# Mirrored RWKV solve, feed-forward loads issued one by one, and another scheduling model in a two-layer hybrid trunk

## The chip, the core and the metric

The kernel runs on one core of a Trainium2 chip. TensorE (PE) multiplies matrices and writes to PSUM; its weight loads (PEld) overlap its matmuls. DVE (VectorE), ACT (ScalarE) and POOL (GpSimd) compute on vectors. DMA engines move data between HBM and SBUF; here nearly all transfers are issued by SP (SyncE). Each engine works through its own queue of instructions in order, and waits where an operand is not ready. The metric is the device time of one execution in microseconds (us), lower is better.

## The reference

Two layers follow each other. In each, 256 tokens of width 1024 are projected by `w_in`; three mixers work on parts of the projection, their outputs are weighted by sigmoid gates and added, and an output projection, a feed-forward block and two layer norms follow. All of it is causal and in float32.

```
p = x @ w_in[l]
y_a = rwkv7_time_mix(p[..., :o_mla], ...)        # 8 heads of 64
y_b = mla_branch(p[..., o_mla:o_s5], ...)        # 8 heads, causal attention
y_c = s5_branch(p[..., o_s5:o_gate], ...)        # 32 groups, 64 states, gelu, GLU
merged = gates[..., 0, :] * y_a + gates[..., 1, :] * y_b + gates[..., 2, :] * y_c
x = layer_norm(DEEPNORM_ALPHA * x + merged @ w_out[l], ln1_g[l], ln1_b[l])
h = jax.nn.silu(x @ ffn_w1[l]) * (x @ ffn_w3[l])
x = layer_norm(DEEPNORM_ALPHA * x + h @ ffn_w2[l], ln2_g[l], ln2_b[l])
```

The RWKV mixer is a recurrence over the tokens. With a state of 64 x 64 per head, one step is

```
sa = jnp.einsum('bhvk,bhk->bhv', state, a_t)
state = state * w_t[:, :, None, :] + sa[..., None] * b_t[:, :, None, :] + v_t[..., None] * k_t[:, :, None, :]
y_t = jnp.einsum('bhvk,bhk->bhv', state, r_t)
```

## The kernel before, in words

**Weights.** All weights come as chunks of 128 x 1024 numbers (512 KB), 138 per layer. `w_load` (L156) issues the transfer into one of three buffers `raw` on SP (L160), rounds the chunk to `whi` on ACT (L161), and forms the remainder `wlo` on DVE (L171; in the first third of a layer a part of it on POOL, L173). There are four pairs of `whi` and `wlo`, and chunks are prepared four ahead of their use. The activations are split in the same way, so that a product in float32 is three matmuls: `xh` with `whi` (L206), `xl` with `whi` (L207) and `xh` with `wlo` (L208). The second projections of a block, with 512 columns, have such triplets at L510 to L512. All of these are called projections here.

**Order.** For each layer two lists, `ORDER1` and `ORDER2`, name the steps in program order: `S` and `r` are projections for S5 and RWKV, `P` and `N` the latents of the attention and their norm, `t` the S5 scan, `p`, `s`, `i`, `j`, `v`, `n` RWKV's preparation, scores, the two parts of the inverse, the solve and the norm, `a` and `b` attention, `l` the GLU and `o`, `h` the outputs of the mixers. From the program the scheduler of the language makes one queue per engine; it may set instructions in another order than the program has them, where the data allow it.

**RWKV.** The eight heads lie in four tiles `f`, two heads to a tile, and two tiles make a pair `g`, in which `e` counts the tiles. `prep` (L858) makes, for one tile, decays and keys: two matmuls (L867, L871), tanh on ACT, scans and products on DVE (L877 to L910, among them `kk`, L893, which reads `pa` from the transposes at L891), transposes of `BK` and `vT` (L916, L921). `scores` (L931) forms `Mk` (L940, copied by ACT, masked by POOL, L947). `inverse` (L951) copies blocks of `Mk` to `P` (on ACT), runs 15 dependent steps of three small DVE operations (L968 to L970), and then builds blocks of 64 (L983 to L1011). `solve` (L1018) has four dependent steps: matmuls of `Mk` with `ST` (L1035, from the second step on with the state, L1031), a copy to `Gc` on ACT, matmuls with the inverse (L1043), a copy into `ST` on DVE, and the update of the state (L1053, L1055, scaled on DVE at L1059). In each step both tiles of the pair use the same rows and columns of the array. L1067 and L1070 then make the output.

**S5.** `s5_tables` (L348) computes tables of powers of the poles; `rotation` runs on POOL, the complex products `cmul` (L404 to L409) on DVE in layer 0, and `spread` (L418, on ACT in layer 0) makes `bd` and `cd`. `s5_in` (L685) copies `u` into the layout `U` with eight transfers (L695) on SP.

**Output projection and second feed-forward projection.** Both are `token_major` (L497), with 8 and 22 chunks. At step `at` of its loop (2 and 12) it issues three transfers on SP: the norm's scale `lg` and shift `lb`, 512 KB each, and the residual `xk`, 1 MB.

The lines of the changed kernel are about 6 higher up to the RWKV part and about 20 higher after it.

## Time and profile before

| | before |
|---|---|
| median of 3 runs | 1072.03 us (1067.92 to 1077.68) |
| the profiled execution | 1068.97 us, its span 1067.1 us |
| PE busy | 1014.2 us, 95% |
| PE weight loads busy | 912.5 us, 86% |
| DVE busy | 784.7 us, 74% |
| ACT busy | 482.6 us, 45% |
| POOL busy | 235.2 us, 22% |
| moved by DMA | 163.86 MB, mean 154 GB/s |

A busy time is the time in which at least one instruction of the engine runs. Matmuls overlap, so the mean time of one is longer than its distance to the next. The page's list of groups has one row for each line, engine and tile: how often, busy us and mean ns, and behind the bar how long the engine stood idle just before them and what ended that. The granted clock (PEclk) is a share of PE's full speed.

### The profile page before, as it was taken

The page shows a single profiled execution, that of the slowest core. Times are in us where ns is not written, and L with a number is a line of the kernel's source. Part 1 is how long each engine was busy: PE and PEld are TensorE (multiplying, and loading weights), DVE is VectorE, ACT ScalarE, POOL GpSimd, SP SyncE. Part 2 cuts the span into 40 slices and gives each one's busy share as a digit, 9 for nine tenths or more (in the row PEclk, how much of TensorE's full clock was granted, in tenths as well). Part 3 has the DMA queues.
Part 4 walks back from the last instruction along what each step waited for, and adds up shares of the span by engine and source line. Part 5 has one row for each costly group of instructions (what it writes and reads, how often), then busy time and mean ns, then how long its engine had stood idle before and what let it go on. Part 6 is the DMA issues. An engine that isn't in the chain of part 4 may idle for free.

```text
span 1067.1 us, 21219 instructions
## 1 busy us (share of the span) xinstructions
PE 1014.2 (95%) x8560; PEld 912.5 (86%) x8560; DVE 784.7 (74%) x1542; ACT 482.6 (45%) x797; POOL 235.2 (22%) x262
## 2 busy tenths in 40 slices
PE   8799989999999999799999999999999999999997
PEld 7798778888896999798878999778889879999885
DVE  7969978976578778386474998888747876667546
ACT  5544477534244244144325346865334423443431
POOL 2970222300000599500012003221002420000000
PEclk9989999999999999999999999999999999999999
DMA  8442241223385555466536325232234755555562
GB/s 280 156 159 90 91 147 41 92 89 100 93 294 177 197 180 171 162 207 217 185 123 218 126 81 191 79 98 85 76 100 173 252 190 215 183 188 183 179 196 79
DMA packets 47394, 163.86 MB, mean 154 GB/s; under 512 B 5696, under 2 KB 8256, under 8 KB 46400
## 3 DMA queue, kind: packets, MB, share of 16 engines
q1 hardware_dynamic: 47008, 161.98, 45.9%
q8 instruction: 67, 1.10, 0.4%
q10 hardware_dynamic: 288, 0.52, 0.1%
q14 instruction: 31, 0.25, 0.1%
HBM read 156.72 MB, written 4.19 MB: 151 GB/s over the span
## 4 chain that ended last, share of the span: by engine, by line
PE 58%; DVE 17%; POOL 9%; DMA 7%; ACT 5%; issue 3%; SPq 0%; DVEq 0%; ACTq 0%; POOLq 0%
PE mm L208 11%; PE mm L207 10%; PE mm L206 10%; DMA raw<-in_ws 6%; DVE wlo L171 3%; PE mm L511 3%; PE mm L512 3%; PE mm L510 3%; ACT whi L161 3%; DVE z L745 1%; PE pa L726 1%; PE pb L1035 1%; POOL st L387 1%; PE pb L1043 1%; PE pa L940 1%
## 5 line engine op out<-in xcount | busy, mean ns | idle before, releaser
L171 DVE TENSOR_TENSOR wlo<-raw,whi 128x1024 fp32r<-128x1024 f32 (+2 forms) x265 | 333.5, 1262 | 171.8 <-ACT whi L161 169.1
L161 ACT CAST whi<-raw 128x1024 fp32r<-128x1024 f32 (+2 forms) x267 | 277.4, 1043 | 379.8 <-PE mm L207 211.8
L206 PE MATMUL mm<-xh,whi 128*128 128x256 f32 x1312 | 376.9, 287 | 14.2 <-ACT whi L161 13.9
L208 PE MATMUL mm<-xh,wlo 128*128 128x256 f32 x1312 | 376.1, 287 | 2.9 <-DVE wlo L171 2.6
L207 PE MATMUL mm<-xl,whi 128*128 128x256 f32 x1312 | 375.1, 286 | 0.4 <-DVE xl L262 0.4
L206 PEld LDWEIGHTS mm<-xh,whi 128*128 128x128 f32 x1312 | 249.2, 190 | 18.6 <-ACT whi L161 14.5
L208 PEld LDWEIGHTS mm<-xh,wlo 128*128 128x128 f32 x1312 | 250.2, 191 | 7.6 <-DVE wlo L171 4.0
L207 PEld LDWEIGHTS mm<-xl,whi 128*128 128x128 f32 x1312 | 250.2, 191 | 2.7 <-DVE xl L262 0.6
L240 POOL TENSOR_TENSOR rs<-rs,mhalf 128x1 f32<-128x1 f32 x8 | 7.8, 971 | 341.2 <-DVE rs L238 341.2
L206 PE MATMUL mm<-yh,whi 128*128 128x256 f32 x256 | 74.6, 291 | 0.1
L207 PE MATMUL mm<-yl,whi 128*128 128x256 f32 x256 | 74.1, 289 | 0.0
L208 PE MATMUL mm<-yh,wlo 128*128 128x256 f32 x256 | 74.1, 289 | 0.0
L511 PE MATMUL mm<-wlo,hh 128*128 128x512 f32 x132 | 52.0, 394 | 0.0
L510 PE MATMUL mm<-whi,hh 128*128 128x512 f32 x132 | 51.7, 394 | 0.0
L512 PE MATMUL mm<-whi,hl 128*128 128x512 f32 x132 | 51.5, 392 | 0.0
L206 PEld LDWEIGHTS mm<-yh,whi 128*128 128x128 f32 x256 | 48.5, 189 | 2.3 <-ACT qa L113 0.9
L207 PEld LDWEIGHTS mm<-yl,whi 128*128 128x128 f32 x256 | 48.5, 190 | 1.2 <-issue 0.8
L208 PEld LDWEIGHTS mm<-yh,wlo 128*128 128x128 f32 x256 | 48.6, 190 | 1.1 <-issue 0.7
L240 POOL TENSOR_TENSOR rsn<-rsn,mhalf 128x8 f32<-128x8 f32 x4 | 6.5, 1634 | 142.8 <-DVE rsn L238 142.8
L173 POOL TENSOR_TENSOR wlo<-raw,whi 128x384 fp32r<-128x384 f32 (+2 forms) x24 | 27.7, 1162 | 44.6 <-ACT whi L161 42.5
L947 POOL TENSOR_SCALAR_AFFINE_SELECT Mk<-Mk 64x512 f32<-64x512 f32 x32 | 27.0, 844 | 43.6 <-ACT Mk L113 42.3
L510 PEld LDWEIGHTS mm<-whi,hh 128*128 128x128 f32 x132 | 24.8, 188 | 6.2 <-DVE th L1284 0.8
(487 smaller groups left out, 1745.7 us busy)
## 6 DMA issues: line engine op xcount, KB each, us to landing
raw<-in_ws SPq DMA_DIRECT2D x267, 512.0 KB, 3.8
raw<-in_ws SPq DMA_DIRECT2D x8, 416.0 KB, 3.5
xd<-xk SPq DMA_DIRECT2D x3, 1024.0 KB, 4.1
xk<-xd SPq DMA_DIRECT2D x3, 1024.0 KB, 7.4
lg<-in_lnv SPq DMA_DIRECT2D x4, 512.0 KB, 5.0
lb<-in_lnv SPq DMA_DIRECT2D x4, 512.0 KB, 5.7
pc<-in_spC SPq DMA_DIRECT2D x2, 768.0 KB, 5.3
pb<-in_spB SPq DMA_DIRECT2D x2, 512.0 KB, 4.9
```

The costliest lines, as they stand in the source:

```text
L161: S.copy(out=hi[:, s], in_=raw[:, s])
L171: V.tensor_tensor(out=lo[:, 0:m], in0=raw[:, 0:m], in1=hi[:, 0:m].bitcast(F32), op=ALU.subtract)
L173: G.tensor_tensor(out=lo[:, m:w], in0=raw[:, m:w], in1=hi[:, m:w].bitcast(F32), op=ALU.subtract)
L206: PE.matmul(ps, lhsT=wh, rhs=xh, start=first, stop=False)
L207: PE.matmul(ps, lhsT=wh, rhs=xl, start=False, stop=False)
L208: PE.matmul(ps, lhsT=wl, rhs=xh, start=False, stop=last)
L240: G.tensor_tensor(out=out, in0=in_, in1=mh(out), op=ALU.pow)
L387: E.tensor_tensor(out=s1, in0=c0, in1=ls, op=ALU.mult)
L510: PE.matmul(acc[b][n], lhsT=ah, rhs=w[0][:, s], start=(k == 0), stop=False)
L511: PE.matmul(acc[b][n], lhsT=ah, rhs=w[1][:, s], start=False, stop=False)
L512: PE.matmul(acc[b][n], lhsT=al, rhs=w[0][:, s], start=False, stop=(k == nk - 1))
L947: G.affine_select(out=Mk[r, h], in_=Mk[r, h], pattern=[[0, 4], [1, 2], [1, 64]], compare_op=ALU.is_ge, fill=0.0, base=-1, channel_multipli ...
```

## The change

There are five parts. In the second list `ORDER1` the projection `r0` moves ahead of `N` and `t0`. The transfers of `U` are issued by ACT instead of SP. `token_major` issues its three loads in another way: in the output projection at the third chunk as before, but under another condition, and in the second feed-forward projection as four transfers at chunks 9 to 12, each tied to follow the chunk's own transfer. The RWKV solve is mirrored: for the second tile of each pair the two halves of the partitions are exchanged in `BK`, `vT`, `ST` and the use of `Mk`, so that its matmuls use other rows and columns of the array than those of the first tile; the transposes of `vT` for that tile become four matmuls with the identity, the copy to `Gc` becomes one of 128 x 128 instead of 64 x 256, and the copy to `ST` is split into one on ACT and one on DVE. Last, the whole program is ordered with `schedule_with_timeline_sim=True`, the scheduler's other model of the machine.

```diff
-    "m S0 S1 P N t0 r0 r1 r2 t1 r3 w0 w1 t2 t3 g0 r4 r5 w2 w3 G3 G1 G2 r6 G0 g1",
+    "m S0 S1 P r0 N t0 r1 r2 t1 r3 w0 w1 t2 t3 g0 r4 r5 w2 w3 G3 G1 G2 r6 G0 g1",
...
-            SY.dma_start(out=raw[:, s], in_=ws[i, :, s])
+            state["dma"] = SY.dma_start(out=raw[:, s], in_=ws[i, :, s])
...
+        loads = [(xk[:, 0], x_dram[:, 0]), (lg, lnv[l, ln:ln + 1, :].to_broadcast([128, D])),
+                 (lb, lnv[l, ln + 1:ln + 2, :].to_broadcast([128, D])), (xk[:, 1], x_dram[:, 1])]
         for k in range(nk - NST):
-            if k == at:
-                SY.dma_start(out=lg, in_=lnv[l, ln:ln + 1, :].to_broadcast([128, D]))
-                SY.dma_start(out=lb, in_=lnv[l, ln + 1:ln + 2, :].to_broadcast([128, D]))
-                SY.dma_start(out=xk, in_=x_dram)
+            if k == 2 and not at:
+                for o, i in loads[1:3] + [(xk, x_dram)]:
+                    SY.dma_start(out=o, in_=i)
             w = w_next()
+            if k in at:
+
+                with tc.issue_after(inst(state["dma"])):
+                    for o, i in loads[at.index(k)::len(at)]:
+                        SY.dma_start(out=o, in_=i)
...
-                        SY.dma_start(out=U2[r:r + 32, j // 2::2, :], in_=u[32 * j:32 * j + 32, :, i, :])
+                        S.dma_start(out=U2[r:r + 32, j // 2::2, :], in_=u[32 * j:32 * j + 32, :, i, :])
...
-                    PE.transpose(ps[:, 128 * b:128 * b + 128], vT[:, f, 128 * b:128 * b + 128], ident)
+                    if e:
+                        for i in range(2):
+                            o = 128 * b + 64 * i
+                            PE.matmul(ps[64 - 64 * i:128 - 64 * i, 128 * b:128 * b + 128], lhsT=vT[:, f, o:o + 64], rhs=ident,
+                                      start=True, stop=True, skip_group_check=True)
+                    else:
+                        PE.transpose(ps[:, 128 * b:128 * b + 128], vT[:, f, 128 * b:128 * b + 128], ident)
                 for i in range(2):
-                    r = slice(64 * i, 64 * i + 64)
+                    r = slice(64 * (i ^ e), 64 * (i ^ e) + 64)
...
-                    rb, rk = slice(64 - 64 * i, 128 - 64 * i), slice(64 * i, 64 * i + 64)
+                    rb = [slice(64 * (1 - i ^ e), 64 * (1 - i ^ e) + 64) for e in range(2)]
+                    rk = rb[::-1]
                     ps = mxps("b")
+                    if b:
+                        for e in range(2):
+                            PE.matmul(ps[rb[e], 0:128], lhsT=ARs[e][:, 0, b, :], rhs=S0[:, e, b - 1], start=True,
+                                      stop=False, skip_group_check=True)
+                    for h in range(2):
+                        o = slice(64 * h, 64 * h + 64)
+                        for e in range(2):
+                            PE.matmul(ps[rb[e], o], lhsT=Mks[e][rk[e], h, b, 0, :], rhs=ST[rk[e], e, c2, i, h, :],
+                                      start=(b == 0), stop=True, skip_group_check=True)
+                    RH = t1("Gc", (128, 4, 65))[:, 0:2, 0:64]
+                    cp(16, out=RH, in_=v2(ps[:, 0:128], 2))
...
                     for e in range(2):
-                        if b:
-                            PE.matmul(ps[rb, 128 * e:128 * e + 128], lhsT=ARs[e][:, 0, b, :], rhs=S0[:, e, b - 1], start=True,
-                                      stop=False, skip_group_check=True)
-                        for h in range(2):
-                            o = 128 * e + 64 * h
-                            PE.matmul(ps[rb, o:o + 64], lhsT=Mks[e][rk, h, b, 0, :], rhs=ST[rk, e, c2, i, h, :],
-                                      start=(b == 0), stop=True, skip_group_check=True)
...
-                    cp(17, out=ST[rb, :, c2, i], in_=ps[rb, 0:256].rearrange("p (e h v) -> p e h v", e=2, h=2))
+                        cp(16 + e, out=ST[rb[e], e, c2, i], in_=v2(ps[rb[e], 0:128], 2))
...
-            token_major(gate0[1], 8, 0, False, q, l, 2)
+            token_major(gate0[1], 8, 0, False, q, l, [])
...
-                token_major((hh, hl), NF, 2, l == layers - 1, q2, l, 12)
+                token_major((hh, hl), NF, 2, l == layers - 1, q2, l, [9, 10, 11, 12])
...
-    with tile.TileContext(nc) as tc:
+    with tile.TileContext(nc, schedule_with_timeline_sim=True) as tc:
```

On PE, the queue of before at the second step of the first solve in layer 0. L206 to L208 are projections; `S_1666` is the state, `ST` and `Gc` the solve's operands.

```order
L1031 MATMUL pb<-S_1666,kr__236 64x128
L1035 MATMUL pb<-ST,Mk 64x64 x2
L1031 MATMUL pb<-S_1666,kr__236 64x128
L1035 MATMUL pb<-ST,Mk 64x64 x2
L206 MATMUL mm<-xh,whi 128x256
L207 MATMUL mm<-xl,whi 128x256
L208 MATMUL mm<-xh,wlo 128x256
L206 MATMUL mm<-xh,whi 128x256
L1043 MATMUL pb<-Gc,DTf_1662 64x64 x4
```

The same place in the queue of the change, where L1052, L1057, L1064, L1075 and L1077 are what L1031, L1035, L1043, L1053 and L1055 were, L960 the scores, L1021 and L1031 the last blocks of the inverse.

```order
L960 MATMUL pa<-kr__236,BK 128x128 x4
L1021 MATMUL pb<-D_2092,Mk 32x32 x16
L1031 MATMUL pb<-DT_2091,P_2093 32x32 x16
L1057 MATMUL pb<-ST,Mk 64x64 x4
L1064 MATMUL pb<-Gc,DTf_1662 64x64 x4
L1077 MATMUL pb<-ST,BKt 64x64 x4
L1052 MATMUL pb<-S_1666,kr__236 64x128 x2
L1057 MATMUL pb<-ST,Mk 64x64 x4
L1064 MATMUL pb<-Gc,DTf_1662 64x64 x4
L1075 MATMUL pb<-S_1666,c 64x64
```

Between the links of the solve stood projections; now the links follow each other, and the next projection comes after the solve and the attention outputs behind it.

On ACT, the queue of before in the first 50 us, where `bd` and `cd` are the S5 tables and `whi` the casts of weight chunks.

```order
L418 ACTIVATE cd<-pb,c 128x32x16 x2
L161 CAST whi<-raw 128x1024
L418 ACTIVATE bd<-pb,c 128x32x16
L593 ACTIVATE kr__236<-mm,dv 128x256
L418 ACTIVATE bd<-pb,c 128x32x16
L593 ACTIVATE kr__236<-mm,dv 128x256
L418 ACTIVATE cd<-pb,c 128x32x16 x2
L593 ACTIVATE kr__236<-mm,dv 128x256
L161 CAST whi<-raw 128x1024
```

And in the change, where L599 is what L593 was.

```order
L113 COPY u<-mm 128x2x128 x2
L701 DMA U_248<-u 32x4x128 x8
L161 CAST whi<-raw 128x1024
L599 ACTIVATE kr__236<-mm,dv 128x256
L161 CAST whi<-raw 128x1024
L418 ACTIVATE bd<-pb,c 128x32x16 x2
L418 ACTIVATE cd<-pb,c 128x32x16 x2
L161 CAST whi<-raw 128x1024
```

The transfers of `U` have come in, and the last `cd` pair is followed at once by a cast, which before had one activation between.

On SP, the queue of before in the feed-forward block of layer 0, from the load of the S5 tables' input `pb` on.

```order
L363 DMA pb<-in_spB 128x1024
L160 DMA raw<-in_ws 128x1024 x23
L516 DMA lg<-in_lnv 128x1024
L517 DMA lb<-in_lnv 128x1024
L518 DMA xk<-xd_4219 128x2048
L160 DMA raw<-in_ws 128x1024 x14
```

And in the change.

```order
L363 DMA pb<-in_spB 128x1024
L160 DMA raw<-in_ws 128x1024 x36
L160 DMA raw<-in_ws 128x832 x2
L160 DMA raw<-in_ws 128x1024 x10
L525 DMA xk<-xd_4233 128x1024
L160 DMA raw<-in_ws 128x1024
L525 DMA lg<-in_lnv 128x1024
L160 DMA raw<-in_ws 128x1024
L525 DMA lb<-in_lnv 128x1024
L160 DMA raw<-in_ws 128x1024
L525 DMA xk<-xd_4233 128x1024
```

The three loads have moved 25 weight chunks back and stand one by one between chunks.

## Rows read from the trace of the kernel before

**Rows 1.** The page: the span, and busy us of each engine with its instructions.
```profile
span 1067.1 us, 21219 instructions
PE 1014.2 (95%) x8560; PEld 912.5 (86%) x8560; DVE 784.7 (74%) x1542; ACT 482.6 (45%) x797; POOL 235.2 (22%) x262
```

**Rows 2.** Waits of PE: who waited for whom, total us, times, longest.
```profile
PE mm L206 <- ACT whi L161: 13.9, 3, 6.8
...
PE pa L726 <- DMA U<-u: 2.3, 1, 2.3
```

**Rows 3.** Stretches of 5 us: length, busy us and instructions per engine, PEclk, DMA.
```profile
45.00:50.00 5.00, 0.73 (x7) 0.53 (x5) 3.63 (x4) 1.33 (x3) 4.92 (x5) 0.84 0.22 86
50.00:55.00 5.00, 2.83 (x11) 2.54 (x12) 4.16 (x5) 3.55 (x6) 5.00 (x4) 0.50 0.20 56
55.00:60.00 5.00, 5.00 (x31) 5.00 (x30) 2.88 (x3) 1.92 (x4) 5.00 (x4) 0.63 0.75 256
...
440.00:445.00 5.00, 5.00 (x44) 5.00 (x44) 0.00 (x0) 0.00 (x0) 2.62 (x3) 1.00 0.24 60
445.00:450.00 5.00, 1.71 (x15) 1.50 (x13) 0.00 (x0) 0.00 (x0) 0.00 (x0) 1.00 0.96 361
450.00:455.00 5.00, 1.00 (x3) 0.71 (x4) 1.49 (x2) 2.35 (x4) 0.00 (x0) 0.62 0.77 313
455.00:460.00 5.00, 5.00 (x31) 5.00 (x32) 4.79 (x10) 2.35 (x3) 0.00 (x0) 0.70 0.60 202
```

**Rows 4.** Timeline of ACT at 48 us: start us, duration, instruction, idle before.
```profile
48.67 1.33 ACT L418 ACTIVATE cd<-pb,c 128x512 f32<-128x512 f32 x2 [4.98 <-DVE pb L408]
...
50.27 1.03 ACT L161 CAST whi<-raw 128x1024 fp32r<-128x1024 f32 x1
```

**Rows 5.** Timeline of SP's DMA issues around 440 us: start us, duration, transfer.
```profile
426.88 0.33 SPq L160 DMA_DIRECT2D raw<-in_ws  x1
442.81 0.33 SPq L516 DMA_DIRECT2D lg<-in_lnv  x1
...
444.18 1.70 SPq L160 DMA_DIRECT2D raw<-in_ws  x3
```

**Rows 6.** One stretch: all engines, then L171 on DVE, then L206 on PE.
```profile
182.30:235.90 53.60, 52.43 (x601) 45.17 (x601) 46.24 (x169) 29.47 (x68) 8.85 (x10) 1.00 0.28 90
...
182.30:235.90 53.60, 10.93 (x9) 1.00 0.28 90
...
182.30:235.90 53.60, 21.78 (x74) 13.83 (x73) 1.00 0.28 90
```

**Rows 7.** Groups of DVE in that stretch: count, busy us, mean ns, idle before.
```profile
L113 DVE COPY ST<-pb 64x256 f32<-64x256 f32 x4 | 1.7, 422 | 4.9 <-PE pb L1043 4.9
...
L968 DVE LOAD_MASK_SELECT s<-DT x22 | 0.3, 13 | 0.4
```

**Rows 8.** Timeline of DVE: the first and the last operation of that stretch.
```profile
182.36 0.48 DVE L893 SCALAR_TENSOR_TENSOR kk<-pa,kr__236 128x256 f32<-128x256 f32 x1
...
235.47 0.42 DVE L113 COPY ST<-pb 64x256 f32<-64x256 f32 x1 [0.90 <-PE pb L1043]
```

**Rows 9.** Timeline of PE in the first step of that solve.
```profile
216.25 0.67 PE L1035 MATMUL pb<-ST,Mk 64*64 64x64 f32 x8
216.86 0.39 PE L207 MATMUL mm<-xl,whi 128*128 128x256 f32 x1
...
218.01 0.68 PE L1043 MATMUL pb<-Gc,DTf 64*64 64x64 f32 x8
```

**Rows 10.** Groups of PE in the whole span: count, busy us, mean ns.
```profile
L1035 PE MATMUL pb<-ST,Mk 64*64 64x64 f32 x128 | 13.3, 229 | 0.0
L1043 PE MATMUL pb<-Gc,DTf 64*64 64x64 f32 x128 | 10.8, 224 | 0.0
```

**Rows 11.** Timeline of ACT in the first step of that solve.
```profile
217.02 0.37 ACT L113 COPY Gc<-pb 64x256 f32<-64x256 f32 x1
217.41 2.45 ACT L113 COPY P<-Mk 32x128 f32<-32x128 f32 x8
```

More of the change, by code (lines that the diff above doesn't have):

```diff
@@ L907, in prep @@
                 b4 = be.rearrange("p (c a) t -> p c a t", c=2)
-                V.scalar_tensor_tensor(out=BK[:, :, 1:3], in0=kk.rearrange("p (c a t) -> p c a t", c=2, a=2), scalar=0.5,
-                                       in1=b4, op0=ALU.mult, op1=ALU.mult)
-                V.tensor_tensor(out=BK[:, :, 0::3], in0=kp.rearrange("p (c a t) -> p c a t", c=2, a=2), in1=b4, op=ALU.mult)
+                inner, outer = BK[:, :, 1:3], BK[:, :, 0::3]
+                k4 = kk.rearrange("p (c a t) -> p c a t", c=2, a=2)
+                if e:
+                    for i in range(2):
+                        V.scalar_tensor_tensor(out=outer[:, i], in0=k4[:, i], scalar=0.5, in1=b4[:, i], op0=ALU.mult,
+                                               op1=ALU.mult)
+                else:
+                    V.scalar_tensor_tensor(out=inner, in0=k4, scalar=0.5, in1=b4, op0=ALU.mult, op1=ALU.mult)
+                V.tensor_tensor(out=inner if e else outer, in0=kp.rearrange("p (c a t) -> p c a t", c=2, a=2), in1=b4,
+                                op=ALU.mult)
                 BKt = t1("BKt", (128, 3, 128), 4)
@@ L920, in prep @@
                 for b in range(2):
-                    PE.transpose(ps[:, 128 * b:128 * b + 128], vT[:, f, 128 * b:128 * b + 128], ident)
+                    if e:
+                        for i in range(2):
+                            o = 128 * b + 64 * i
+                            PE.matmul(ps[64 - 64 * i:128 - 64 * i, 128 * b:128 * b + 128], lhsT=vT[:, f, o:o + 64], rhs=ident,
+                                      start=True, stop=True, skip_group_check=True)
+                    else:
+                        PE.transpose(ps[:, 128 * b:128 * b + 128], vT[:, f, 128 * b:128 * b + 128], ident)
                 for i in range(2):
-                    r = slice(64 * i, 64 * i + 64)
+                    r = slice(64 * (i ^ e), 64 * (i ^ e) + 64)
                     cp(8, out=ST[r, :, i], in_=ps[r, 0:256].rearrange("p (c h v) -> p c h v", c=2, h=2))
@@ L959, in inverse @@
                         cp(10, out=P32[r, 4 * e:4 * e + 4].rearrange("p (h c) t -> p h c t", h=2),
-                               in_=Mks[e][r, :, 1 - i // 2::2, 0, 32 * (i % 2):32 * (i % 2) + 32])
+                               in_=Mks[e][r, :, (1 - i // 2) ^ e::2, 0, 32 * (i % 2):32 * (i % 2) + 32])
                 N16, DT, s16, t16 = (t1(n, (128, 8, 16)) for n in ("N16", "DT", "s16", "t16"))
@@ L1001, in inverse @@
                         PE.matmul(ps[r2, 32 * m:32 * m + 32],
-                                  lhsT=Mks[m // 4][r, m // 2 % 2, 2 * (m % 2) + 1 - i // 2, 0, 32:64],
+                                  lhsT=Mks[m // 4][r, m // 2 % 2, 2 * (m % 2) + ((1 - i // 2) ^ (m // 4)), 0, 32:64],
                                   rhs=D32[r, m, :], start=True, stop=True, skip_group_check=True)
@@ L1037, in solve @@
-                    RH = t1("Gc", (128, 4, 65))[:, :, 0:64]
-                    cp(16, out=RH[rb], in_=v2(ps[rb, 0:256], 4))
-                    ps = mxps("b")
-                    for e in range(2):
-                        for h in range(2):
-                            o = 128 * e + 64 * h
-                            PE.matmul(ps[rb, o:o + 64], lhsT=DTf[rb, 4 * e + 2 * h + c2, :], rhs=RH[rb, 2 * e + h, :],
-                                      start=True, stop=True, skip_group_check=True)
@@ new lines, in solve @@
+                    RH = t1("Gc", (128, 4, 65))[:, 0:2, 0:64]
+                    cp(16, out=RH, in_=v2(ps[:, 0:128], 2))
+                    ps = mxps("b")
+                    for h in range(2):
+                        for e in range(2):
+                            PE.matmul(ps[rb[e], 64 * h:64 * h + 64], lhsT=DTf[rb[e], 4 * e + 2 * h + c2, :],
+                                      rhs=RH[rb[e], h, :], start=True, stop=True, skip_group_check=True)
+                    for e in range(2):
+                        cp(16 + e, out=ST[rb[e], e, c2, i], in_=v2(ps[rb[e], 0:128], 2))
```

## The prediction, made before the changed kernel had run

> **What bounds the kernel now.** I read the page's busy times first: TensorE (PE) is busy 1014.2 of 1067.1 us, DVE 784.7 [rows 1]. A change therefore pays where it fills one of PE's 53 us of gaps, and costs where it opens a new one. Next I read the list of PE's waits: the largest is for the weight casts on ACT, 13.9 us in three waits, the longest 6.8; the one wait for the U transfer is 2.3 us [rows 2]. Then I cut the span into stretches of 5 us and counted matmuls. Where nothing is missing, 5 us hold 44 projection matmuls of 256 columns (440 to 445), 0.1136 us each [rows 3]. Two places fall far short. From 45 to 60 us there are 7, 11 and 31: 83 of 132 are missing, 83 x 0.1136 = 9.4 us. From 445 to 460 there are 15, 3 and 31: again 83, 9.4 us [rows 3]. The reader should see that the granted clock falls with them, to 0.50 and 0.62, so that PE also restarts slowly.
>
> The first gap is a queue behind a blocked instruction: on ACT the two `cd` activations (L418) begin at 48.67 after 4.98 us of waiting for DVE's `pb` (L408), and the cast of the next weight chunk stands behind them and starts at 50.27 [rows 4]. The second is on SP: it issues `raw` at 426.88, then `lg` not before 442.81, then `lb` and `xk`, and the next `raw` at 444.18 [rows 5]. For 17 us no weights are ordered, and then 2 MB stand in front of them.
>
> Last I looked at a place that loses nothing, because the order changes it most: in layer 0 the piece from the `kk` of the third RWKV tile (of four, two heads each) on DVE (182.36) to the last `ST` copy of the first solve (235.47) [rows 8]. In these 53.6 us PE is busy 52.4, and 3 x 74 - 1 = 221 of its 601 matmuls are projections [rows 6], put between the links of the chain.
>
> **The change, part by part.** *Spaced feed-forward loads.* In the second projection `xk`, `lg`, `lb` and the rest of `xk` now go out one by one, each behind a weight chunk, and (by the order of SP) 25 chunks later than before. POOL's table, for which `lg` waited, is long done then. The 9.4 us come back; if one 512 KB load still delays a chunk by its own time, about 1.5 us of DMA at the 361 GB/s of 445 to 450 [rows 3], four of them leave 4. In the output projection the opposite happens: `lg`, `lb`, `xk` stand together in both layers. 2 MB at that rate are 5.8 us; four weight chunks are prepared ahead, at 24 matmuls x 0.1136 = 2.7 us or more each, 10.9 us of cover, so I cost it at nothing; without that cover it is 5.8 us per layer.
>
> *The start.* In the new order of ACT the last `cd` pair stands one chunk cast later, and on DVE the operations that feed it are no longer interrupted by two token-shift steps of about 0.5 us. One chunk more of cover is 2.7 us, the earlier `cd` about 2.6: of the wait of 6.8 some 1.5 remain, and with it the low clock goes. Gain 7 us; bounds 4 (the longer cover alone and some of the clock) and 9.4.
>
> *U.* The eight U transfers leave SP for ACT, and in layer 1 projection `r0` now stands ahead of `t0`, which waited 2.3 us [rows 2]. I take 3 with the restart, bounds 2.3 and 3.7. ACT carries eight issues of about 0.4 us; it is idle more than half the time [rows 1], which hides them; uncovered they would be 3.3 us per layer.
>
> *Mirrored tiles.* The matmuls of a pair's two tiles now use different quadrants of the array in each step. L1035 and L1043 keep PE busy 13.3 and 10.8 us in the kernel [rows 10]; eight take 0.61 us (216.25 to 216.86) [rows 9]. Where PE is the limit, which is the second solve of each layer, that is half, 12 us; if pairs ran wholly together 6 would be saved. I take 4, bounds 0 and 6. The copies get smaller or split in two; I cost them at nothing, since DVE and ACT hide them, and 0.1 us a step if not.
>
> Gains: 9.4 + 7 + 3 + 4 = 23.4 us; bounds 4 + 4 + 2.3 + 0 = 10.3 and 28.5.
>
> *The order.* The rows of PE show the price. In the new order the projections come first, then a run of 266 matmuls in layer 0 and 270 in layer 1 in which no projection stands: the last two tiles' preparation, the inverse and the first pair's four solve steps. DVE has no weight difference (`wlo`) in 140 rows there, ACT no cast in 35. PE works in order, so what it waits for in this run is not filled. How long does the run last? It begins when PE has written `pa` for the third tile, since DVE's `kk` reads it, and PE has only 12 projections (1.4 us) left then. To the last `ST` copy DVE has 152 operations, one of them a `wlo`. In the same piece before, DVE did 169: 9 `wlo` in 10.93 us, 22 mask selects in 0.3 [rows 6, 7], and 138 others in 46.24 - 10.93 - 0.3 = 35.0, 0.254 us each. So 151 x 0.254 + 1.2 = 39.5 us if DVE never waits. Before it was idle 53.6 - 46.24 = 7.4 us, 4.9 of them for the solve's matmuls [rows 6, 7]; with these it is 46.9. I take 45, near the upper end: the chain goes to and fro between PE, ACT and DVE, and on ACT eight copies `P` of 2.45 us together stand ahead of the next `Gc`, as they did before [rows 11].
>
> PE's own work in it: 52.43 less 221 x 0.1136 = 27.3 us, or, if a projection between two links costs 0.144 (eight from 216.86 to 218.01 [rows 9]), 20.6. I take 22, since the run has no such changes. PE is then idle 45 - 22 - 1.4 = 21.6 us per layer; bounds 39.5 - 27.3 - 1.4 = 10.8, and 46.9 - 20.6 - 1.4 + 3 = 28, the 3 for attention's output behind the run, where ACT's cast is still to come. Two layers: 43 us, bounds 22 and 56. Nothing gives it back: PE's total work in the zone is the same, and afterwards it is as full as before.
>
> A rule can be set beside this. The rows say that 221 projections x 0.1136 = 25.1 us lay between the links and PE lost 1.2 of 53.6 us [rows 6]. The Trainium skill, Perfetto Trace Analysis, section Optimization Strategy, says that where the most-contended engine changes over time, interleaving the regimes may help; that speaks against this change, which takes them apart. If all that was interleaved is paid again, the two layers lose 50 us and the sum is 1069 + 50 - 23 = 1096 instead of the 1089 below.
>
> **Sum.** 1069 + 43 - 23 = 1089 us. The profiled execution took 1069, 3 us under the median of three, 1072, and within their spread of 1068 to 1078; I give the sum as it is.
>
> **Rivals.** *The run is covered after all: faster.* If DVE were so far ahead that PE found its inputs ready, the run would cost nothing and 1069 - 23 = 1046 would be left. It decides at 23.4 / 2 = 11.7 us of idle time per layer. For it speaks that the lower bound is 10.8. Against it speaks that the run's first DVE operation needs a matmul that stands only 1.4 us ahead of it, so no lead can have been built up.
>
> *No change: the order closes other gaps too.* PE's gaps are 53 us; the places above account for some 20. If the new order recovered 20 of the rest, the sum would be 1069. Nothing I found in the rows does this, but 8000 rows of PE differ.
>
> *Slower still: the clock.* After 5 us without work the granted clock was 0.50, the lower of two levels, 1.2 of 2.4 GHz [rows 3]. If the run's gaps bring it down, PE's share in the solve steps, some 8 us of the 22, doubles: 8 us per layer more, 1105; with the 2 MB of the output projection uncovered, 12 more, 1117.
>
> *The tiles do not run side by side.* Then 4 us are missing: 1093.
>
> **How the numbers follow.** My case has 0.62, with a range of its own of 1069 + 22 - 28 = 1063 to 1069 + 56 - 10 = 1115; the covered run 0.13, other gaps 0.11, the clock and the burst 0.14; the side-by-side question and the sum by the rule lie within the first. The predicted time is 1089. The range from 1057 to 1116 leaves out most of the covered run and the far end of the clock, under 2 in 10. One per cent is 10.7 us, about what a measurement of this kernel can tell from no change: slower means above 1083. My case lies above that in two thirds of its weight, the clock always; no change takes the rest of my case and the other gaps: faster 0.14, same 0.27, slower 0.59.
>
> **What would show it.** Right: in both layers a stretch of about 45 us without projections in which PE is busy about half and waits for DVE's and ACT's solve copies; 445 to 460 and the start without their gaps; no PE wait for the U transfer. Wrong: PE's busy share stays at 95% there, or the waits for `whi` at the start stay at 13.9 us. The price falls if DVE's operations in the run take less than 40 us, and rises if the granted clock there is 0.5.

## The result, and the profile after

The changed kernel took 1154.9 us (median of four runs, 1152.1 to 1159.8), the kernel before 1073.6 beside it: a ratio of 1.075, interval 1.070 to 1.080. It is slower by 81 us. The direction was forecast, the size was not: the forecast was 1089, with a range to 1116.

First the page of the changed kernel: the span, the busy times, and the clock of TensorE in 40 slices. They answer to [rows 1].

```profile
span 1155.5 us, 21313 instructions
PE 1044.7 (90%) x8584; PEld 937.7 (81%) x8584; DVE 791.5 (69%) x1546; ACT 485.3 (42%) x813; POOL 229.8 (20%) x262
PEclk9999889956997899999989999997599799999998
```

Two things grew. PE is idle for 1155.5 - 1044.7 = 110.8 us instead of 52.9. And it is busy 30.5 us longer, although the mirrored tiles add only 24 records to its 8560. The clock row shows why: a pit of 5 and 6 in the ninth and tenth slice (231 to 289 us), another in the 28th and 29th (780 to 838 us). The mean granted clock is 0.926 where it was 0.986. With levels of 1 and 0.5 that is 2 x (1 - 0.926) x 1155.5 = 171 us at the lower level, against 30.

Next, the stretches in which the place can be seen: start to end, length, busy us and instructions of PE, weight loads, DVE, ACT, POOL, then the clock and the DMA. The first row is the end of attention's first part up to the first tile, the second the first two tiles, the third and sixth the run from the third tile to the first solve's output (one per layer), the fourth and seventh the tail behind the second solve, the fifth the projection with the spaced loads.

```profile
118.80:160.10 41.30, 31.47 (x349) 25.97 (x350) 29.44 (x64) 20.15 (x36) 11.88 (x14) 0.83 0.18 59
160.10:220.60 60.50, 60.50 (x452) 54.93 (x451) 41.20 (x82) 34.50 (x75) 6.54 (x12) 1.00 0.37 123
220.60:278.70 58.10, 39.55 (x435) 29.88 (x434) 40.92 (x185) 19.07 (x56) 5.73 (x9) 0.56 0.06 19
343.70:368.90 25.20, 16.06 (x91) 14.01 (x90) 16.98 (x28) 5.75 (x7) 2.83 (x7) 0.73 0.55 194
414.30:532.00 117.70, 117.70 (x1035) 117.42 (x1035) 94.35 (x121) 50.85 (x67) 81.27 (x88) 1.00 0.54 174
781.90:837.10 55.20, 39.71 (x454) 29.89 (x453) 43.51 (x192) 21.09 (x63) 5.75 (x9) 0.66 0.06 20
900.30:925.50 25.20, 17.08 (x97) 15.29 (x97) 17.39 (x27) 8.08 (x10) 6.81 (x5) 0.73 0.53 188
```

The same stretches of before, in the same order, without those of layer 1:

```profile
109.70:145.60 35.90, 29.69 (x310) 24.83 (x309) 31.58 (x63) 21.91 (x38) 12.66 (x13) 1.00 0.36 111
145.60:180.70 35.10, 35.07 (x238) 29.46 (x238) 27.88 (x64) 23.16 (x59) 6.55 (x12) 1.00 0.28 91
180.70:237.60 56.90, 55.73 (x647) 48.40 (x647) 49.22 (x186) 30.59 (x71) 8.85 (x10) 1.00 0.26 85
281.80:319.60 37.80, 36.37 (x298) 35.97 (x298) 27.08 (x36) 16.39 (x20) 4.07 (x7) 1.00 0.72 242
358.90:488.00 129.10, 121.65 (x1046) 120.36 (x1045) 90.76 (x121) 50.65 (x67) 82.09 (x88) 0.97 0.53 179
```

The run is there as forecast: 58.1 us with PE busy 39.55, 55.2 with 39.71, so 18.5 and 15.5 us idle. But it passes at a clock of 0.56 and 0.66. Before, the same piece took 56.9 us *and* held some 200 more matmuls; these now stand ahead of it, in the second row, where PE has not a single gap for 60.5 us while DVE is busy 41.2. The tail behind the second solve had 298 matmuls and 1.4 us idle; now it has 91, and 9.1 us idle. The spaced loads do what they should: 117.7 us where 129.1 stood.

The waits of PE answer to [rows 2]: who waited for whom, total us, times, longest.

```profile
PE pa L490 <- DVE xk L483: 9.5, 2, 5.1
PE mm L208 <- DVE wlo L171: 9.1, 3, 5.6
PE pc L1116 <- DVE yT L1111: 8.6, 2, 5.8
PE pb L1064 <- ACT Gc L113: 8.4, 8, 2.9
PE pa L930 <- DVE BK L919: 6.8, 2, 5.6
PE pa L930 <- DVE s L988: 5.1, 1, 5.1
```

The 13.9 us for `whi` are gone from the top. In their place stand the layer norm (`xk`, 9.5 us where it was 0.6), 9.1 us for `wlo`, the tail's `yT`, the solve's `Gc`, the tile's `BK` and DVE's shuffles of the inverse (`s`). The first three lie outside the runs.

### The profile page after: what moved, and what is told of

Read it like the earlier page. It is cut to its first block, busy times and chain, and to the rows that moved or that the text cites. A ratio compares the mean times of both kernels' runs of the same rounds, so it can differ in the third digit from the quotient of the medians.

```text
span 1155.5 us, 21313 instructions
## 1 busy us (share of the span) xinstructions
PE 1044.7 (90%) x8584; PEld 937.7 (81%) x8584; DVE 791.5 (69%) x1546; ACT 485.3 (42%) x813; POOL 229.8 (20%) x262
## 4 chain that ended last, share of the span: by engine, by line
PE 72%; DVE 14%; ACT 5%; DMA 5%; issue 3%; POOL 1%; DVEq 0%; ACTq 0%; SPq 0%; POOLq 0%
PE mm L206 15%; PE mm L208 15%; PE mm L207 15%; DMA raw<-in_ws 4%; PE mm L511 3%; PE mm L510 3%; PE mm L512 3%; DVE wlo L171 2%; ACT whi L161 1%; PE pa L732 1%; PE pa L960 1%; PE pa L1210 1%; POOL wlo L173 1%; PE pc L511 1%; PE pc L512 1%
## 5 line engine op out<-in xcount | busy, mean ns | idle before, releaser
L171 DVE TENSOR_TENSOR wlo<-raw,whi 128x1024 fp32r<-128x1024 f32 (+2 forms) x265 | 331.8, 1256 | 225.7 <-ACT whi L161 223.7
L208 PE MATMUL mm<-xh,wlo 128*128 128x256 f32 x1312 | 376.4, 287 | 9.3 <-DVE wlo L171 9.1
L206 PE MATMUL mm<-xh,whi 128*128 128x256 f32 x1312 | 376.8, 287 | 3.9 <-ACT whi L161 1.5
L208 PEld LDWEIGHTS mm<-xh,wlo 128*128 128x128 f32 x1312 | 249.6, 190 | 13.4 <-DVE wlo L171 9.9
L206 PEld LDWEIGHTS mm<-xh,whi 128*128 128x128 f32 x1312 | 250.9, 191 | 10.1 <-issue 2.4
L206 PE MATMUL mm<-yh,whi 128*128 128x256 f32 x256 | 75.2, 297 | 8.6 <-DVE yh L113 2.5
L208 PE MATMUL mm<-yh,wlo 128*128 128x256 f32 x256 | 75.5, 296 | 0.0
L206 PEld LDWEIGHTS mm<-yh,whi 128*128 128x128 f32 x256 | 50.4, 199 | 11.9 <-DVE yh L113 4.0
L173 POOL TENSOR_TENSOR wlo<-raw,whi 128x384 fp32r<-128x384 f32 (+2 forms) x24 | 33.9, 1412 | 95.0 <-ACT whi L161 92.9
L208 PEld LDWEIGHTS mm<-yh,wlo 128*128 128x128 f32 x256 | 50.6, 198 | 1.4 <-issue 0.5
L207 PEld LDWEIGHTS mm<-yl,whi 128*128 128x128 f32 x256 | 50.6, 198 | 0.1
L510 PE MATMUL mm<-whi,hh 128*128 128x512 f32 x132 | 47.6, 392 | 0.0
L967 POOL TENSOR_SCALAR_AFFINE_SELECT Mk<-Mk 64x512 f32<-64x512 f32 x32 | 21.7, 679 | 62.7 <-ACT Mk L113 61.5
L512 PEld LDWEIGHTS mm<-whi,hl 128*128 128x128 f32 x132 | 24.8, 188 | 5.6
```

What stands on the lines that cost most here:

```text
L171: V.tensor_tensor(out=lo[:, 0:m], in0=raw[:, 0:m], in1=hi[:, 0:m].bitcast(F32), op=ALU.subtract)
L173: G.tensor_tensor(out=lo[:, m:w], in0=raw[:, m:w], in1=hi[:, m:w].bitcast(F32), op=ALU.subtract)
L206: PE.matmul(ps, lhsT=wh, rhs=xh, start=first, stop=False)
L207: PE.matmul(ps, lhsT=wh, rhs=xl, start=False, stop=False)
L208: PE.matmul(ps, lhsT=wl, rhs=xh, start=False, stop=last)
L510: PE.matmul(acc[b][n], lhsT=ah, rhs=w[0][:, s], start=(k == 0), stop=False)
```

## The experiments

All ran with a kernel before on the same chip; ratios are to that. I began by splitting the change.

**The order alone**

```diff
-    with tile.TileContext(nc) as tc:
+    with tile.TileContext(nc, schedule_with_timeline_sim=True) as tc:
```

> The kernel before with schedule_with_timeline_sim=True and nothing else. Theory O (the order alone is the loss): its queues hold the same uncovered runs as the changed kernel's (218 and 197 matmuls without a projection), so 1073 + 70 to 95 = 1143 to 1168 us, about 160 us of the span at the lower clock, FFN1 of layer 0 with its gap or without it depending on where the loads come to stand. Rival M (the mirrored solve or the moved transfers bring a good part of it): under 1120 us.

It took 1179.6 us, ratio 1.100 (1.094 to 1.107), more than expected: the order costs over 100 us by itself. The changed kernel, with the same flag, took 25 us less; so under this order the other parts are worth more than the 11 us that the next run shows without it.

**All but the order**: the changed kernel without that flag.

> The changed kernel without schedule_with_timeline_sim, so with the scheduler's usual model. Theory O: no run without projections is left, so the parts show their gains: spaced loads 9, U with r0 3, mirrored tiles 4, together 1073 - 16 = 1057 us, bounds 1045 to 1068. Rival M: 1085 us or more, with PE waits in the solve.

It took 1063.6 us, ratio 0.990 (0.987 to 0.993). Its page, and from the third tile to the first solve's output, then the tail behind the second solve:

```profile
span 1060.7 us, 21288 instructions
PE 1010.1 (95%) x8584; PEld 908.8 (86%) x8584; DVE 784.7 (74%) x1546; ACT 485.1 (46%) x813; POOL 236.6 (22%) x262
...
182.90:238.30 55.40, 54.36 (x662) 47.40 (x661) 49.56 (x188) 31.26 (x75) 7.33 (x10) 1.00 0.28 91
274.30:317.60 43.30, 41.67 (x343) 41.34 (x343) 30.94 (x39) 18.70 (x24) 4.06 (x7) 1.00 0.70 240
```

This is the best ground for comparison, since it executes the same 8584 PE records as the changed kernel. The order makes 1155.5 - 1060.7 = 94.8 us by the spans: 60.2 are PE's idle time (110.8 against 50.6), 34.6 are the same matmuls taking longer (1044.7 against 1010.1). By the medians, 1154.9 and 1063.6, it is 91.

**The spaced loads alone**

```diff
-            if k == at:
-                SY.dma_start(out=lg, in_=lnv[l, ln:ln + 1, :].to_broadcast([128, D]))
-                SY.dma_start(out=lb, in_=lnv[l, ln + 1:ln + 2, :].to_broadcast([128, D]))
-                SY.dma_start(out=xk, in_=x_dram)
...
+            if k in at:
...
+                with tc.issue_after(inst(state["dma"])):
+                    for o, i in loads[at.index(k)::len(at)]:
+                        SY.dma_start(out=o, in_=i)
```

> The kernel before with the loads of token_major in the new form and nothing else. If the 17 us without weight orders at 427 to 444 us are what empties PE there, PE's 7.5 us of gaps in FFN1 of layer 0 and the lower clock behind them go: 1073 - 9 = 1064 us, bounds 1060 to 1069. If the gap has another cause (POOL's table), it stays and the time is 1070 to 1076. The output projection's three loads in one place may cost up to 6 us per layer.

1064.1 us, ratio 0.992 (0.988 to 0.996): as expected. The gap at 445 to 460 us of [rows 3] is filled; two of its three slices:

```profile
445.00:450.00 5.00, 5.00 (x44) 5.00 (x43) 3.72 (x6) 1.67 (x2) 0.00 (x0) 1.00 0.73 212
450.00:455.00 5.00, 5.00 (x44) 5.00 (x43) 3.93 (x6) 1.77 (x3) 0.00 (x0) 1.00 0.68 209
```

**The mirrored tiles alone**: `rb`, `rk`, the mirrored columns of `BK`, `Mk` and `ST`, and the copies that belong to them.

> The kernel before with the mirrored RWKV tiles and nothing else. If the two tiles' 64x64 matmuls run side by side, L1035 and L1043 (now L1057 and L1064) fall from 24.1 us busy to 12 to 18, and the time to 1060 to 1069 us. If they run one after the other, their busy time stays at 24 and the time at 1070 to 1076.

1072.2 us, ratio 0.998 (0.994 to 1.002): no difference that can be told. Yet the matmuls do run side by side, against 13.3 and 10.8 in [rows 10]:

```profile
L1058 PE MATMUL pb<-Gc,DTf 64*64 64x64 f32 x128 | 7.2, 230 | 0.0
L1051 PE MATMUL pb<-ST,Mk 64*64 64x64 f32 x128 | 7.2, 230 | 0.0
```

The mean of one matmul stays 230 ns, but the time in which PE is busy with them falls from 24.1 to 14.4 us: pairs overlap. The output projection of layer 0 ends 6.1 us earlier, but 3.6 of these were won ahead of the first tile, where nothing is mirrored. And it is lost again in layer 1, from S5's first matmuls (L726) on. The first row is of this kernel, the second of the kernel before:

```profile
577.00:618.10 41.10, 40.78 (x326) 37.31 (x327) 29.44 (x61) 12.39 (x18) 0.00 (x0) 0.80 0.34 111
```
```profile
581.60:615.60 34.00, 33.67 (x326) 30.89 (x327) 28.60 (x61) 12.51 (x18) 0.00 (x0) 1.00 0.42 132
```

The same 326 records take 7.1 us longer without a longer wait: PE is full in both, and the granted clock is 0.80 instead of 1.00. Just ahead of them PE waited 3.1 us for `U`, before 2.3. So the profiled runs can't tell what the mirrored tiles are worth by themselves.

**A bare run in the usual order.** The order is a single flag that moves thousands of instructions, so I made its most visible feature alone. In the kernel with all but the order, every projection that the program has after the first solve is held behind that solve (`hold` is its last matmul):

```diff
+        hold = state.get("hold")
+        with tc.issue_after(inst(hold)) if hold is not None else ExitStack():
             for k in range(nk):
...
```

> Everything of the change but the order, and one hold: every matmul of a projection that stands in the program after solve 0 is queued behind solve 0's last matmul. This makes a run of 214 matmuls without a projection in layer 0 and of 196 in layer 1 (217 and 199 in the changed kernel, none over 60 in the kernel with all but the order, which took 1063.6 us), while the rest of the order stays the usual one. Theory A, the bare run is the main cause: as in the changed kernel, 15 to 18 us idle and the low clock throughout each run, with some 28 to 37 us of PE work at half speed (14 to 18 us lost), so 25 to 35 us per layer, 1115 to 1135 us; the tails behind the second solve stay covered, since the projections come later than before. Theory B, the loss is that of many small places of the other order (start, tails, LN) and the run costs only its idle time: 1064 + 2 x 10 = 1084 us or less. If it is 1064 to 1070 the run costs nothing at all.

1105.0 us, ratio 1.024 (1.019 to 1.029). It lies between the two theories: 41 us more than without the hold, or 37 by the ratios, since the two ran on different chips; some 20 per layer. By spans, 1103.2 - 1060.7 = 42.5 us: 26.5 are idle time (PE busy 1026.1 of 1103.2), 16.0 are longer matmuls. The two halves of each run, tiles and then inverse with solve, in both layers:

```profile
184.60:211.00 26.40, 13.92 (x79) 9.96 (x78) 21.89 (x107) 10.03 (x28) 3.30 (x6) 0.60 0.07 20
211.00:241.50 30.50, 24.11 (x382) 19.57 (x381) 18.56 (x81) 11.15 (x36) 2.64 (x4) 0.68 0.01 2
721.90:750.00 28.10, 20.98 (x136) 15.31 (x139) 26.09 (x111) 12.76 (x33) 4.12 (x7) 0.75 0.11 38
750.00:778.00 28.00, 22.57 (x366) 17.95 (x357) 15.44 (x67) 10.60 (x34) 2.64 (x4) 0.64 0.01 2
```

In these stretches lie 31 us of PE's idle time and, by 2 x (1 - clock) x length, 75 us at the lower clock. In the two runs of the changed kernel it is 34 and 88. So a run without projections is a cause, and it costs nearly the same under the usual order as under the other; but it accounts for less than half of what the order costs. Outside the runs PE idles 46 us here, 49 without the hold, and 77 in the changed kernel.

**Cover given back to the solve.** The changed kernel, with the projections of two work lists queued behind the first step of the first solve.

```diff
+        hold = state.get("hold") if state.get("tok", "-") in "oh" else None
+        with tc.issue_after(inst(hold)) if hold is not None else ExitStack():
             for k in range(nk):
...
```

> The changed kernel with its order, but the projections of two of its work lists (the ones that feed the gate and the last tile) queued behind the first step of solve 0: the solve has 32 to 68 projection matmuls between its steps again, and bare runs of 170 (layer 0) and 128 (layer 1) matmuls stay ahead of it. Theory A, cover is what the order took away: the solve itself is back at full clock and hides its round trips, the tails get some cover, 15 to 30 us off, 1125 to 1140 us; the time at the low clock falls from 164 us to 120 or less. Theory B, the loss isn't in the run: 1150 to 1160 us.

1153.9 us, ratio 1.071 (1.065 to 1.076): no gain that can be told. The solve itself was covered, as theory A has it: from its first to its last `ST` copy in layer 0 PE idles 0.6 us instead of 3.8, and 4.9 us are at the lower clock instead of 14.2. But the bare stretch ahead of it still idles 15.5 us (14.8 in the changed kernel), and PE idles 107.8 us in all (busy 1043.5 of 1151.3), 3 less than in the changed kernel. So the time of theory A failed: the solve is the smaller part of the run.

**The waits filled with matmuls that help nothing**

```diff
+    def warm(ps, n, c=384):
+        for _ in range(n):
+            PE.matmul(ps[:, c:c + 128], lhsT=ones, rhs=ones, start=True, stop=True, skip_group_check=True)
...
```

> The changed kernel with matmuls of a constant by itself (128x128, type f32, some 0.21 us each at the full clock) in the waits of the bare run: 16 ahead of the BK transposes of each of the last two tiles, 4 behind each of the first two block products and behind the two products of each of the four steps of solve 0; 72 per layer, 15 us of PE work at the full clock and 31 us at half; the order of the other instructions stays nearly the same. They help nothing but the clock. Theory A, the clock falls because PE waits in the run, and half its loss is the clock: the granted clock in the run rises well over 0.5, the run's own work (28 to 37 us of busy time at half) gets 10 to 18 us shorter per layer, which pays for the dummies that lie in waits or more: 1135 to 1160 us. Theory B, the clock stays at 0.5 whatever fills the waits: the dummies cost 31 us less the 15 to 18 us of waits they fill, per layer: 1175 to 1190 us.

1165.9 us, ratio 1.081 (1.076 to 1.087). The runs, by the same landmarks as the third and sixth row of the changed kernel:

```profile
217.30:284.20 66.90, 54.60 (x579) 45.69 (x579) 41.52 (x186) 19.27 (x57) 5.89 (x9) 0.74 0.05 17
778.90:843.50 64.60, 53.38 (x598) 44.84 (x597) 44.06 (x192) 20.94 (x63) 5.80 (x9) 0.84 0.05 18
```

The clock rises from 0.56 to 0.74 and from 0.66 to 0.84, so it does follow PE's waits, against theory B; but the time is no shorter, against theory A (the intervals of the two ratios overlap). What it is worth can be read at one group, the tiles' score matmuls. The first row is of the run in the changed kernel, the second of the filled run, the third of the kernel with all but the order, where the clock is 1.00:

```profile
L960 PE MATMUL pa<-kr__236,BK 64*128 64x128 f32 x32 | 7.2, 438 | 0.0
```
```profile
L965 PE MATMUL pa<-kr__236,BK 64*128 64x128 f32 x32 | 4.6, 328 | 0.0
```
```profile
L960 PE MATMUL pa<-kr__236,BK 64*128 64x128 f32 x32 | 4.6, 285 | 0.0
```

The same 32 records are 2.6 us longer at the lower clock. But the fillers keep PE busy for 49.8 us themselves (two groups, 32.3 and 17.5), more than the waits that they fill (idle time 91.9 instead of 110.8), and ACT's `ST` copies now wait 17.6 us behind them. A clock that is bought with empty work gave nothing back here.

**Cover spread over the run.** Now with the changed kernel's order again: 240 projection matmuls are dealt out over the last two tiles, the block products and the solve.

```diff
+            an, n = state.get("an"), state.get("n", 0)
+            hold = an[n * len(an) // state["tot"]] if an and n < state["tot"] else None
...
+            with tc.issue_after(inst(hold)) if hold is not None else ExitStack():
...
```

> The changed kernel with its order, but the first 80 eighths of projections (240 matmuls) that the program has after solve 0 are handed out evenly over the run: each is queued behind one of some 16 matmuls of the last two tiles, of the block products and of the steps of solve 0. So 15 to 30 projection matmuls stand at nearly every place of the run where PE waited, no run of over 69 matmuls is bare, and the projections ahead of the first two tiles are fewer by the same number. Theory A, the order loses by spending the cover early: the run's 15 to 18 us idle and its 37 to 51 us at the low clock go down to under 4 and 10, the tails behind the second solve stay as in the changed kernel; 30 and 25 us off, 1095 to 1115 us. Theory B, what the order costs lies in its other places (start, tails, LN, feed-forward) and in what DVE does in the run, which no cover mends: 1135 to 1155 us. What is left above the 1064 us of the usual order is the price of the order's other places.

1142.9 us, ratio 1.066 (1.058 to 1.075), a number of theory B. As the shares were coarse, with 24 matmuls at one group of each solve step and none at the others, I ran a **finer spread**, three matmuls at a time, with more ahead of the longer waits:

> As the kernel with the cover spread (1142.9 us), but in finer shares: three projection matmuls at a time, 21 behind the first transposes of each of the last two tiles, six behind the BK transposes, the block products, and behind each of the three groups of a step of solve 0 (there it had 24 at one group of each step and none at the one in front of the wait for Gc). In the kernel with the coarse spread the time at the low clock in layer 0's run fell from 51 us to some 20, but PE stayed idle for about 18 us in it. Theory A, idle time in the run is cover in the wrong places: with the fine spread the run's idle time falls under 6 us and the low clock under 10 us per layer, 20 to 30 us off the coarse spread's time, 1115 to 1125 us. Theory B, the waits are DVE's own lateness in this order (its tile work queued behind the 45 instructions of the inverse), which cover behind the wait can't fill: 1138 to 1145 us again.

1138.2 us, ratio 1.060 (1.053 to 1.067), theory B's number. From the second tile to the inverse, then the solve:

```profile
178.00:232.00 54.00, 40.12 (x401) 30.92 (x401) 41.49 (x157) 26.84 (x75) 9.02 (x16) 0.87 0.06 20
232.00:265.00 33.00, 30.64 (x287) 26.50 (x286) 22.18 (x84) 12.01 (x27) 0.00 (x0) 0.79 0.21 66
```

The solve is covered (30.6 of 33.0), and the clock in the tiles is 0.87. But ahead of it PE still loses 13.9 us, and there neither DVE (41.5 of 54) nor ACT (26.8) is full: they wait too. Together the 87 us hold 684 PE records. Without the flag the same piece is this row, with more of them; by the landmarks, from the second tile's `kk` to the last `ST` copy, it is 68.0 us there and 78.9 here:

```profile
168.30:238.30 70.00, 68.94 (x757) 58.74 (x756) 60.71 (x216) 41.99 (x101) 10.64 (x16) 1.00 0.27 88
```

**Projections later.** In the last try they were also taken away from between the first and the third tile (48 instead of 144), so that DVE's tile work isn't behind them.

> The changed kernel with its order, but the projections that the program has from the third tile on stand behind the third tile's own matmuls, three at a time: between the first and the third tile there are 48 projection matmuls instead of 144 (fine cover, 1138.2 us), the last two tiles and the block products have a bare run of 116 (128 in layer 1), the solve's groups have nine each, and the tail behind the second solve has 77 or more. In the fine-cover kernel DVE was busy 15.4 of 21, 15.2 of 22 and 18.1 of 20 us while PE worked off the 144, where the usual order keeps it at 17 of 17. Theory A, projections put first hold up DVE's work on the tiles, and that is the part of the loss that cover in the run can't give back: the third tile starts some 20 to 30 us earlier, the first solve ends 15 to 25 us earlier, the tail's idle time of 6 to 9 us goes, and the whole takes 1100 to 1125 us although a bare run is back. Theory B, a bare run costs what it costs wherever it stands: 1135 to 1155 us.

1140.5 us, ratio 1.057 (1.052 to 1.061): theory B again. The third tile's transposes start at 191.5, against 195.7 in the fine cover, not 20 to 30 us earlier; against the changed kernel the third tile's `kk` comes 28 us earlier (193.1, 221.0) and the first solve ends 17.5 us earlier, and still the time fell by 14 only. The tail idles 1.7 and 3.9 us instead of 9.1 and 8.1, but with the bare run back PE idles 47 us from the first tile to the first solve's end, both layers together; it was 34 in the changed kernel, 34 and 31 with the coarse and the fine cover. DVE's largest waits from the end of the first part to the first solve, of which none stands out:

```profile
DVE wlo L171 <- ACT whi L161: 6.7, 4, 4.6
DVE bon L956 <- PE pa L955: 6.6, 4, 2.4
DVE N L991 <- ACT P L113: 6.3, 2, 4.4
DVE Pt L1230 <- PE pa L1227: 5.5, 5, 2.0
```

**A version that beats both kernels.** The usual order with the spaced loads and the mirrored tiles; U stays on SP and the first work list as it was.

> The usual order with the spaced feed-forward loads and the mirrored tiles alone: U goes back to the SyncE queue and the first list of work to its old place. A version that may beat both kernels: spaced loads alone took 1064.1 us, mirrored tiles alone 1072.2, all but the order 1063.6. If the parts add up: 1060 us (1055 to 1064). If the mirrored tiles give nothing however they are combined: 1064 to 1066.

1060.7 us, ratio 0.983 (0.977 to 0.989). Its interval overlaps that of all but the order (0.987 to 0.993), so U on ACT and the new list bring nothing that these runs can tell.

## Why the prediction failed

**The spaced loads: right.** 9.4 forecast; alone they made 8 (0.992, interval 4 to 13 us), and the stretch is 11.4 us shorter.

**The start: wrong.** I gave it 7 us, because the last `cd` would no longer hold up the casts. The wait for `whi` did shrink, but DVE is now the late one: in the stretches that answer to 45 to 60 us of [rows 3] it is busy throughout.

```profile
45.00:50.00 5.00, 3.52 (x29) 3.31 (x29) 5.00 (x4) 2.24 (x3) 4.92 (x5) 1.00 0.52 173
50.00:55.00 5.00, 1.59 (x22) 1.18 (x20) 5.00 (x5) 1.35 (x3) 4.92 (x5) 1.00 0.08 31
55.00:60.00 5.00, 2.77 (x13) 2.77 (x14) 5.00 (x5) 3.11 (x5) 4.92 (x3) 0.58 0.33 106
```

There are 64 matmuls where 49 were, of 132, and PE waits 9.1 us for `wlo`. The kernel with all but the order has that wait too, 8.7 us. I had named the stall that was to go, but not what is late next.

**U and `r0`: no gain to be seen.** The wait is 1.8 us (2.3 before), but 3.6 with all but the order, and the version without these edits is no slower.

**The mirrored tiles: side by side as forecast, the gain not seen.** I put 4 us, between 0 and 6, counting the second solves alone. Over both solves PE's busy time fell from 24.1 to 14.4 us; alone they made no difference in time that can be told (-2 to 7 us). In the sum of gains stood 23; without the order they are 11, of which the loads make 8. The missing 12 are one term of the miss, the start above all.

**The run: its mechanism was right, its clock was not in the sum.** Idle time was forecast as 21.6 per layer; it is 18.5 and 15.5. DVE's own work was put at 39.5 us; it is 40.9. But from `kk` of the third tile (221.0) to the last `ST` copy (276.4) it takes 55 us, and 52 in layer 1, not 45; and PE's own work, put at 22, is busy for 35. The idle time came out near the forecast because both were too small. I had set the fall of the clock aside as a rival at 0.14, with 16 us. It came, through most of both runs, and on all of PE's work in them, where I had priced the solve's share alone. The two runs hold 88 of the 171 us at the lower level (2 x (1 - clock) x length: 51 and 37), against none of 34 in the kernel with all but the order. In the bare run of the usual order 75 such us made the matmuls 16.0 us longer; by that rate the 88 make some 19 of the 34.6 us that the order adds to the busy time, an estimate.

**"Nothing gives it back ... afterwards it is as full as before": this step failed.** I argued that PE's total work in the zone is the same, so only the run could lose. But the projections are one stock: those that stand ahead of the run are missing behind it as well. The tail behind the second solve had 298 matmuls and has 91; it idles 9.1 and 8.1 us instead of 1 to 3, and its clock is 0.73. Ahead of the first tile 9.8 us are idle instead of 6.2. At the layer norms PE waits 9.5 us for `xk`; in the seven kernels with the flag this wait is 7.3 to 11.4 us, in those without it at most 0.6. In all, of the 60 us that the order adds to PE's idle time, 32 lie in the two runs and 28 elsewhere. With the longer matmuls that is some 51 us in the runs, where 43 were forecast, and some 44 us elsewhere, where nothing was.

**Cover put back does not buy the price back.** In the usual order a bare run costs 20 us per layer, close to the 21.6 that I forecast, but by luck: 13 of them are idle time and 8 the clock. In the changed order cover dealt back in three ways recovers 12 to 17 of the 91 us that the order costs (10 to 20 by the ratios). It takes 12 to 43 us off the time at the lower clock between the first tile and the first solve's end (84 us in both layers), and nothing or next to nothing off PE's idle time there. The other engines' queues were reordered too, and I took that for the rest. From the end of the first part to the end of the first solve, DVE waits for ACT's casts thus, in the changed kernel and in the one with all but the order:

```profile
DVE wlo L171 <- ACT whi L161: 19.6, 12, 4.6
```
```profile
DVE wlo L171 <- ACT whi L161: 1.7, 2, 1.3
```

An instance, from DVE's timeline in the changed kernel (start, duration, instruction, idle before it):

```profile
153.81 0.42 DVE L923 TENSOR_TENSOR BK<-kp,uu 128x256 f32<-128x256 f32 x1 [0.84 <-ACT uu L891]
158.81 1.23 DVE L171 TENSOR_TENSOR wlo<-raw,whi 128x1024 fp32r<-128x1024 f32 x1 [4.58 <-ACT whi L161]
160.51 0.48 DVE L899 SCALAR_TENSOR_TENSOR kk<-pa,kr__236 128x256 f32<-128x256 f32 x1 [0.47 <-PE pa L897]
```

A weight difference stands ahead of the first tile's `kk` and waits 4.58 us for its cast. But this wait holds up nothing: `kk` then waits another 0.47 us for PE, whose transposes stand behind more than 30 projection matmuls without a gap, though their input was ready at 153.6:

```profile
160.09 0.38 PE L897 MATMUL pa<-c,kr 128*128 128x128 f32 x2
```

PE is busy during every one of the 19.6 us, and in the run itself only this is left of them:

```profile
DVE wlo L171 <- ACT whi L161: 0.2, 1, 0.2
```

With the projections later they fell to 6.7 us, and the time was no better than with cover alone. So these waits of DVE are not the missing price; the tile waited for its place in PE's own queue.

**What stays open.** That the early projections make the 44 us outside the runs too is argued from the tails and not shown: no experiment gave the tails, the layer norms or the start their cover back by itself. Nor is it shown why PE's idle time between the tiles outlasts the cover, 9 to 16 us from the third tile to the first `ST` copy in every one of those tries against 1.0 and 0.6 without the flag. The experiments moved PE's projections and left the queues of DVE and ACT in the flag's order. A kernel with the flag's order on PE alone and the usual one on DVE and ACT, or the reverse, would tell more, and was not tried.

**The rivals.** That the run is covered (1046) and that other gaps close (1069) are refuted by idle times of 18.5 and 15.5 us and by 110.8 in all. The clock with the burst (1105 to 1117) had the right mechanism; no burst was seen in the output projection, where PE idles 0.7 us in layer 0 and 0.9 in layer 1. The rule that I set beside the sum, from the Trainium skill, Perfetto Trace Analysis, section Optimization Strategy, pointed the right way: the bare run alone, which does nothing but take the regimes apart, cost 37 to 42 of the 50 us worked out there, and the whole order 91, since the tails and the clock were not in them either.

## What to carry to other kernels

Work that fills another chain's waits is a stock: when an order spends it early, count what is missing in every later place as well as in the chain, and put the lower clock on every matmul of an uncovered stretch. Before a long wait on another engine is called a cause, look whether the bound engine was idle during it: here 19.6 us of such waits fell where PE had no gap. And where one flag moves thousands of instructions, measure it apart from the rest of a change: here the rest was worth 1 to 2 per cent, and the flag hid it.

## What the runs showed of the hardware

The granted clock fell to its lower level in stretches where PE was far from still. In the first row PE is busy 15.86 of 20 us, and the clock is at 0.50 throughout:

```profile
240.00:260.00 20.00, 15.86 (x237) 12.04 (x237) 8.23 (x29) 9.09 (x28) 2.64 (x4) 0.50 0.01 2
260.00:280.00 20.00, 14.55 (x156) 11.20 (x157) 15.68 (x77) 2.99 (x11) 0.00 (x0) 0.56 0.01 1
```

It had fallen in a stretch, 222 to 230 us, in which PE was busy 2.8 of 8 us, and came back only at the end of the run. I had taken the low clock for the companion of an idle PE; here it stayed with one that was busy three quarters of the time. In the kernel with the mirrored tiles alone it stayed at 0.50 from 580 to 593 us, where PE was busy without a gap. And two 64x64 matmuls in different quarters of the array overlapped: 14.4 us of busy time instead of 24.1 for the same 256 records.
